# Late attention's scores in pieces of at most 512 columns, in two one-bank PSUM tiles, with a longer assumed delay of key loads

## Chip, cores, metric

One core of a Trainium2 (trn2) chip. The metric is the device time of one execution in microseconds; the kernel before was timed in three runs.

## The reference

One layer of a streaming encoder. The part that matters here is the differential attention of the prompt: 2048 frames behind 16 meta tokens, 4 heads, two softmax maps per head whose difference weights the values. A query may see every key of its own 64-frame chunk and of all earlier ones.

```python
def diff_attend(q, k, v, lam, mask):
    s = jnp.einsum('...qhcd,...khcd->...hcqk', q, k).astype(jnp.float32) * (HEAD_DIM_A ** -0.5)
    if mask is not None:
        s = jnp.where(mask, s, -jnp.inf)
    p = jax.nn.softmax(s, axis=-1)
    a = p[..., 0, :, :] - lam * p[..., 1, :, :]
    return jnp.einsum('...hqk,...khe->...qhe', a.astype(v.dtype), v)
...
    hx = hx + mix_out(oa_x, ob_x, gb_x, lw, li)
    hx = hx + ffn(hx, lw)
```

Around it stand the input projection, a gated linear attention (GLA), eight running streams of 16 frames (the sample), the output projection `mix_out` and a SwiGLU feed-forward network (FFN) of width 2816. All tensors are fp32.

## The kernel before, in words

Every product that must be exact to fp32 is made of rounded parts (`fp32r`): a high part and a low part of each operand, three products of 512 columns each (`mm3`, L203; L75 is the one line that issues all matmuls, L79 the transposes).

**Order of the work.** TensorE's (PE's) and SyncE's (SP's) instructions stand in an order that a planner in the program makes (class `Order`, L56). Streams of work are generators; each yields what it waits for next: a number of us, an event plus a delay, or a slot of a named resource. The planner keeps a virtual clock, which matmuls and transposes advance (and which jumps ahead when nothing is ready), and always goes on with the highest-ranked stream whose condition holds by that clock. The constants at L38 to L47 are the delays that it assumes. They make no instruction wait; they decide how much other PE work stands between two steps. On the chip the engines wait for each other through semaphores, and each engine runs its own instructions in order. The order on VectorE (DVE), ScalarE (ACT) and GpSimd (POOL) is made by the framework's scheduler.

**Two main streams.** `stream()` (L567) does the four projections, half of the output projection, and then the FFN in four groups of tokens, A1, A2, B1, B2 (L616 to L625). `attention()` (L533) does the sample, then the prompt's attention in three instances of class `Attention`: query blocks 0 to 3 (528 keys), blocks 4 to 7 (1040 keys), and, once the projections are done, blocks 8 to 15 (2064 keys). This last one, the late attention (L1557), runs beside the output projection, the last GLA units and the FFN of A1 and A2; after it comes the second half of the output projection, for which B1 waits.

**One unit of attention** is a head h and a block i of 128 queries; W = 16 + 128(i+1) keys. `scores` (L800) cuts W into pieces of at most 1024 columns, in each of the two maps m: blocks 8 to 14 have two pieces of 584, 648, ... 968 columns, block 15 has three of 688. Each piece takes the slot "S" of the planner, whose assumed time of use is `lat[0]`, and the PSUM tile `S`, 1024 columns wide (two banks), of which there is one:

```python
                for b, (c0, c1) in enumerate(pieces):
                    yield ("res", "S", self.lat[0])
                    S = self.ps.tile([P, 1024], F32, tag="S", bufs=1, name=f"S{h}_{i}_{m}_{b}")
```

PE writes the piece as chunks of up to 512 columns, two products a chunk (with the keys' high part `kh` and low part `kl`), and in the unit's last piece of a map one of 64 columns that masks (`big`, `ind`). Then DVE takes the row's minimum (L827) and ACT the exponential with the row sum (L828, followed by a read of the accumulator). Only then may the next piece overwrite `S`. `combine` (L834) brings the pieces to one maximum: eight small operations on `st`, then for each piece one ACT scaling of map 1 (L857) and one DVE sum into map 0 (L858). `output` (L862) comes `lat[1]` later: transposes (`at`), copies by ACT (L883) and products with the values (`ao`). A unit's scores wait until the output of the unit two before is done (`pbufs`, L898).

**Keys.** `load_k` (L761) issues eight DMAs for a head and map (two halves of the keys, high and low part, each into both halves of the partitions) and posts an event; the first scores of that map stand at least `L_KS` = 2.37 of virtual time behind it (L814). The keys of the next head are loaded when block 15 has been issued.

**FFN.** The gate and up products go into PSUM tiles `pg` and `pu`, one of each; weights come by DMA into `wrg`, `wru`, `wrd`, are rounded by ACT (L1398) and their rest is taken by POOL (L1399); `pd` is the down product, added to `h` by DVE (L1459). `tph` are the transposes of a group's normed input `hn`.

Of the kernel before, what the change touches and what calls it, by code (L numbers as in the profile page):

```python
# [9 lines left out]
F32 = mybir.dt.float32  # L10
# [9 lines left out]
P = 128  # L20
# [17 lines left out]
L_G0 = 14.55  # L38
L_G = 2.77, 2.08, 2.69
L_E = 4.5, 9.94, 1.75  # L40
L_L = 4.19, 12.69, 2.7
L_Y, L_Y0 = 9.97, 17.89
L_H = 2.66
L_V, L_Q, L_KS = 2.89, 2.08, 2.37
L_W, L_ST, L_STX, L_GP, L_GL = 0.68, 2.12, 2.19, 2.49, 5.29
L_K, L_K0 = 2.1, 0.92
L_TR, L_X, L_QK, L_KD, L_FTR = 3.13, 1.82, 12.48, 5.25, 2.97  # L47
# [8 lines left out]
class Order:  # L56
# [8 lines left out]
    def matmul(self, out, lhsT, rhs, **kw):  # L65
        n = 1
        for d in list(out.shape)[1:]:
            n *= d
        m = lhsT.shape[-1]
        if lhsT.dtype == F32R:  # L70
            self.now += max(n / 2400, m / 1200)
        else:
            c = max(n / 600, m / 600)
            self.now += c / 4 if "tile_position" in kw else c
        self.nc.tensor.matmul(out, lhsT, rhs, **kw)  # L75
# [52 lines left out]
def hymba_kernel(ctx: ExitStack, tc: tile.TileContext, I: dict, O: dict, stop: int = 9):  # L128
# [3 lines left out]
    order = Order(nc)  # L132
# [614 lines left out]
    class Attention:  # L747


        def __init__(self, pool, ps, nk, blocks, pbufs, vbufs, lat):  # L750
            self.pool, self.ps, self.nk, self.blocks = pool, ps, nk, blocks
            self.pbufs, self.vbufs, self.lat = pbufs, vbufs, lat
            self.k, self.q, self.vs = {}, {}, {}
            self.ready = {}
            self.vmz = pool.tile([P, 512], F32, name=f"vmz{nk}")
            nc.gpsimd.memset(self.vmz, 0.0)
            dma(self.vmz[0:NMETA], new_v[0:NMETA])
            self.qseq = [(h, g) for h in range(H) for g in range(blocks[0] // 2, blocks[-1] // 2 + 1)]
            self.units = [(h, i) for h in range(H) for i in blocks]
# [40 lines left out]
        def scores(self, h, i):  # L800
            pm = self.pool
            q = self.q[h, i // 2][:, :, (i % 2) * P:(i % 2 + 1) * P]
            W = NMETA + (i + 1) * P
            np_ = -(-W // 1024)
            step = -(-W // np_)
            pieces = [(c, min(c + step, W)) for c in range(0, W, step)]
            st = pm.tile([P, 40], F32, tag="st", bufs=4, name=f"st{h}_{i}")
            mn = st[:, 0:2 * np_].rearrange("p (m b) -> p m b", m=2)
            sm = st[:, 6:6 + 2 * np_].rearrange("p (m b) -> p m b", m=2)
            yield ("ev", ("q", self.nk, h, i // 2), L_Q)  # L810
            pr = [pm.tile([P, self.nk], F32, tag=f"p{m}", bufs=self.pbufs[m], name=f"p{m}_{h}_{i}")
                  for m in range(2)]
            for m in range(2):
                yield ("ev", ("k", self.nk, h, m), L_KS)  # L814
                kh, kl = self.k[h, m]
                for b, (c0, c1) in enumerate(pieces):
                    yield ("res", "S", self.lat[0])
                    S = self.ps.tile([P, 1024], F32, tag="S", bufs=1, name=f"S{h}_{i}_{m}_{b}")
                    for a0 in range(c0, c1, 512):
                        a1 = min(a0 + 512, c1)  # L820
                        m0 = max(a0, W - CHUNK)
                        o = S[:, a0 - c0:a1 - c0]
                        matmul(o, q[:, m, :], kh[:, a0:a1], start=True, stop=False)
                        matmul(o, q[:, m, :], kl[:, a0:a1], start=False, stop=m0 >= a1)
                        if m0 < a1:
                            matmul(S[:, m0 - c0:a1 - c0], ind, big[:, 0:a1 - m0], start=False, stop=True)
                    nc.vector.tensor_reduce(out=mn[:, m, b:b + 1], in_=S[:, 0:c1 - c0], axis=AX.X, op=ALU.min)  # L827
                    nc.scalar.activation(pr[m][:, c0:c1], S[:, 0:c1 - c0], AF.Exp, bias=mn[:, m, b:b + 1],  # L828
                                         scale=-1.0, accum_out=sm[:, m, b:b + 1])
                if i == self.blocks[-1] and h + 1 < H:  # L830
                    spawn(self.load_k(h + 1, m), 0, ("att", self.nk))
            return pieces, st, mn, sm, pr, W

        def combine(self, ctx_):  # L834
            pieces, st, mn, sm, pr, W = ctx_
            np_ = len(pieces)
            if np_ == 1:
                rz, r = st[:, 12:14], st[:, 14:15]
                nc.vector.reciprocal(rz, sm.rearrange("p m b -> p (m b)"))
                nc.vector.scalar_tensor_tensor(out=r, in0=sm[:, 0, :], scalar=nlam, in1=rz[:, 1:2],  # L840
                                               op0=ALU.mult, op1=ALU.mult)
                nc.vector.scalar_tensor_tensor(out=pr[0][:, 0:W], in0=pr[1][:, 0:W], scalar=r, in1=pr[0][:, 0:W],
                                               op0=ALU.mult, op1=ALU.add)
                return pr[0], rz[:, 0:1]
            mo, z, rz = st[:, 12:14], st[:, 14:16], st[:, 16:18]
            f = st[:, 18:18 + 2 * np_].rearrange("p (m b) -> p m b", m=2)
            fz = st[:, 24:24 + 2 * np_].rearrange("p (m b) -> p m b", m=2)
            nc.vector.tensor_reduce(out=mo, in_=mn, axis=AX.X, op=ALU.min)
            nc.vector.tensor_tensor(out=f, in0=mo.unsqueeze(2).to_broadcast([P, 2, np_]), in1=mn, op=ALU.subtract)
            nc.scalar.activation(f, f, AF.Exp)  # L850
            nc.vector.tensor_tensor(out=fz, in0=f, in1=sm, op=ALU.mult)
            nc.vector.tensor_reduce(out=z, in_=fz, axis=AX.X, op=ALU.add)
            nc.vector.reciprocal(rz, z)
            nc.vector.tensor_tensor(out=rz, in0=rz, in1=lamv, op=ALU.mult)
            nc.vector.tensor_tensor(out=f, in0=f, in1=rz.unsqueeze(2).to_broadcast([P, 2, np_]), op=ALU.mult)
            for b, (c0, c1) in enumerate(pieces):
                nc.scalar.activation(pr[1][:, c0:c1], pr[1][:, c0:c1], AF.Identity, scale=f[:, 1, b:b + 1])  # L857
                nc.vector.scalar_tensor_tensor(out=pr[0][:, c0:c1], in0=pr[0][:, c0:c1], scalar=f[:, 0, b:b + 1],  # L858
                                               in1=pr[1][:, c0:c1], op0=ALU.mult, op1=ALU.add)
            return pr[0], ones  # L860
# [51 lines left out]

        def run(self):
            g = ("att", self.nk)
            order.slots("S", 1)
            spawn(self.all_outputs(), 2, g)
            spawn(self.all_scores(), 1.5, g)
            yield ("idle", g)
# [600 lines left out]
    def pools(name, side):  # L1519
        return (tc.alloc_tile_pool(name=name, bufs=1, side=side),  # L1520
                tc.alloc_tile_pool(name=name + "_ps", bufs=1, space=PSUM, side=side))
# [11 lines left out]
    def attention():  # L1533

        yield ("ev", ("proj", 0), 4.0)
        pm, ps = pools("smp", "left")
        yield from make_sample(pm, ps)
        close(ps, pm, qbp)
        glap, glaps = pools("gla", "left")
        gl[:] = [glaps, glap]  # L1540
        spawn(make_gla(glap, [lambda nm: glaps.tile([P, 512], F32, tag="b1", bufs=1, name=nm)]), 2, "gla")
        pm, ps = pools("att0", "left")
        yield from Attention(pm, ps, NMETA + 512, list(range(4)), pbufs=(3, 2), vbufs=2,
                             lat=L_E).run()
        close(ps, pm)
        pm, ps = pools("att1", "left")
        yield ("ev", ("proj", 1), 6.0)
        yield from Attention(pm, ps, NMETA + 1024, list(range(4, 8)), pbufs=(3, 1), vbufs=3,
                             lat=L_E).run()
        close(ps, pm)  # L1550
        po, pps = pools("outa", "left")
        po2s[:] = [po]
        outa[:] = po, pps, output_projection(po, pps, 1, first, out_weights(po, 1, first, 1, 4.0), 2, 1, 2, po2s)
        post("early")
        yield ("ev", ("px",), 4.0)
        pm, ps = pools("att", "right")
        yield from Attention(pm, ps, NMETA + SEQ, list(range(8, NT)), pbufs=(2, 1), vbufs=4,  # L1557
                             lat=L_L).run()
        close(ps, pm)
        po, pps = pools("outb", "right")  # L1560
        for part in (1, 0):
            w = out_weights(po, part, second, 4, 3.0)
            yield from output_projection(po, pps, part, second, w, 3, 1, 2)
        close(pps, po)
        post("outb")
# [113 lines left out]
```

## Time and profile before

| | us |
|---|---|
| median of three runs | 3137.93 (3133.88 to 3143.64) |
| the profiled execution | 3135.83 |
| its span, first to last instruction | 3134.0 |
| PE busy | 2988.7 |
| DVE busy | 1463.4 |
| ACT busy | 1210.4 |
| mean granted clock of TensorE | 0.982 of full |

The profile is of one execution. Its page gives each engine's busy time, the chain of work that ended last and groups of instructions; the trace behind it answers for any stretch: who waited for whom, the instructions in order of time, and busy times with the granted clock. A wait is idle time of an engine just before an instruction, put down to what released it. The late attention lies between 977 us (its first score) and 1906 us.

### The profile page before, as it was taken

The numbers are of one execution on the slowest core, as the hardware profiler recorded it, in microseconds if no ns is written. First come the engines' busy times: TensorE is split into PE (matmuls) and PEld (weight loads), VectorE is DVE, ScalarE is ACT, GpSimd is POOL, SyncE is SP. The second block draws the span as 40 slices with busy tenths as digits, with TensorE's granted clock in tenths as the row PEclk, the third lists the DMA queues.
The fourth block names the chain that finished last, engine by engine and source line by source line (L and its number), as shares of the span: only waits on it lengthen the run. The fifth ranks groups of instructions, "written<-read, shape, count | busy, mean of one in ns | idle before, by whom it ended". The sixth has DMA issues, their size and how long they took to land. (4 is left out here: it accounts for less than half of the span.)

```text
span 3134.0 us, 41977 instructions
## 1 busy us (share of the span) xinstructions
PE 2988.7 (95%) x16049; PEld 2492.6 (80%) x16049; DVE 1463.4 (47%) x2506; ACT 1210.4 (39%) x2270; POOL 953.5 (30%) x530
## 2 busy tenths in 40 slices
PE   8999999999998896999999999999999999999999
PEld 5776778787776785887877887788788877999998
DVE  6445346556653653544445654643333333333333
ACT  5444434455541544544434543322322223222221
POOL 2012112122251102323322335424444444333332
PEclk9999999999998998999999999999999999999999
DMA  4437676546368437225234324643333334322222
GB/s 158 126 129 221 215 212 174 172 149 190 105 215 207 144 131 196 88 68 136 74 80 137 127 72 149 200 161 108 121 122 93 100 109 133 102 73 77 81 69 73
DMA packets 411358, 415.22 MB, mean 132 GB/s; under 512 B 34547, under 2 KB 303029, under 8 KB 411157
## 3 DMA queue, kind: packets, MB, share of 16 engines
q1 hardware_dynamic: 372372, 384.26, 40.5%
q10 hardware_dynamic: 38528, 28.26, 2.8%
q8 instruction: 127, 2.08, 0.3%
q14 instruction: 75, 0.61, 0.1%
q0 software_dynamic: 256, 0.01, 0.0%
HBM read 334.02 MB, written 78.42 MB: 132 GB/s over the span
## 5 line engine op out<-in xcount | busy, mean ns | idle before, releaser
L1459 DVE TENSOR_TENSOR h<-h,pd 128x512 f32<-128x512 f32 x374 | 255.9, 685 | 460.5 <-PE pd L75 460.0
L1399 POOL TENSOR_TENSOR wgl<-wrg,wgh 128x1024 fp32r<-128x1024 f32 x88 | 216.4, 2459 | 497.8 <-PE pu L75 343.2
L1399 POOL TENSOR_TENSOR wul<-wru,wuh 128x1024 fp32r<-128x1024 f32 x88 | 214.2, 2434 | 447.7 <-PE pg L75 335.8
L75 PE MATMUL pg<-nh,wgh 128*128 128x512 f32 (+1 forms) x880 | 324.7, 369 | 6.8 <-DVE sg L201 6.8
L75 PE MATMUL pu<-nh,wuh 128*128 128x512 f32 (+1 forms) x880 | 321.8, 366 | 0.0
L75 PE MATMUL pg<-nl,wgh 128*128 128x512 f32 (+1 forms) x880 | 318.1, 361 | 0.0
L75 PE MATMUL pg<-nh,wgl 128*128 128x512 f32 (+1 forms) x880 | 317.5, 361 | 0.0
L75 PE MATMUL pu<-nl,wuh 128*128 128x512 f32 (+1 forms) x880 | 315.9, 359 | 0.0
L75 PE MATMUL pu<-nh,wul 128*128 128x512 f32 (+1 forms) x880 | 315.6, 359 | 0.0
L75 PE MATMUL pd<-wdh,th 128*128 128x512 f32 x748 | 296.8, 397 | 5.4 <-DVE h L1459 4.2
L75 PE MATMUL pd<-wdh,tl 128*128 128x512 f32 x748 | 293.6, 393 | 0.0
L75 PE MATMUL pd<-wdl,th 128*128 128x512 f32 x748 | 292.4, 391 | 0.0
L827 DVE TENSOR_REDUCE st<-S 128x1 f32<-128x688 f32 (+13 forms) x208 | 179.6, 863 | 223.7 <-PE S L75 222.0
L828 ACT ACTIVATE p<-S,st 128x688 f32<-128x688 f32 (+13 forms) x208 | 172.3, 829 | 230.2 <-DVE st L827 228.5
L1399 POOL TENSOR_TENSOR wdl<-wrd,wdh 128x1024 fp32r<-128x1024 f32 x88 | 225.9, 2567 | 102.6 <-ACT wdh L1398 102.4
L1448 ACT CAST th<-sg 128x512 fp32r<-128x512 f32 (+1 forms) x110 | 61.3, 557 | 403.2 <-DVE sg L1446 403.1
L75 PEld LDWEIGHTS pg<-nh,wgh 128*128 128x128 f32 x880 | 167.1, 190 | 29.6 <-DVE sg L201 8.0
L75 PEld LDWEIGHTS pg<-nh,wgl 128*128 128x128 f32 x880 | 166.6, 189 | 23.4
L75 PEld LDWEIGHTS pg<-nl,wgh 128*128 128x128 f32 x880 | 167.1, 190 | 21.2
L75 PEld LDWEIGHTS pu<-nh,wul 128*128 128x128 f32 x880 | 165.1, 188 | 22.5
L75 PEld LDWEIGHTS pu<-nh,wuh 128*128 128x128 f32 x880 | 165.3, 188 | 21.1
L75 PEld LDWEIGHTS pu<-nl,wuh 128*128 128x128 f32 x880 | 165.5, 188 | 20.7
(396 smaller groups left out, 6358.8 us busy)
## 6 DMA issues: line engine op xcount, KB each, us to landing
wrg<-in_w_ffn_gate_dram SPq DMA_DIRECT2D x88, 512.0 KB, 4.0
wru<-in_w_ffn_up_dram SPq DMA_DIRECT2D x88, 512.0 KB, 3.9
wrd<-in_w_ffn_down_dram SPq DMA_DIRECT2D x88, 512.0 KB, 3.4
h_d<-xr SPq DMA_DIRECT2D x34, 512.0 KB, 3.8
xr<-h_d SPq DMA_DIRECT2D x17, 512.0 KB, 4.0
hn<-h_d SPq DMA_DIRECT2D x17, 512.0 KB, 4.5
h<-h_d SPq DMA_DIRECT2D x17, 512.0 KB, 7.0
out_dram<-h SPq DMA_DIRECT2D x17, 512.0 KB, 3.1
```

The source lines that it names most:

```text
L75: self.nc.tensor.matmul(out, lhsT, rhs, **kw)
L827: nc.vector.tensor_reduce(out=mn[:, m, b:b + 1], in_=S[:, 0:c1 - c0], axis=AX.X, op=ALU.min)
L828: nc.scalar.activation(pr[m][:, c0:c1], S[:, 0:c1 - c0], AF.Exp, bias=mn[:, m, b:b + 1], scale=-1.0, accum_out=sm[:, m, b:b + 1])
L1399: nc.gpsimd.tensor_tensor(out=b, in0=raw, in1=r32(a), op=ALU.subtract)
L1448: nc.scalar.copy(th[:, c0:c0 + n], sg)
L1459: nc.vector.tensor_tensor(out=hs[n][:, e], in0=hs[n][:, e], in1=ps, op=ALU.add)
```

## The change

Late attention gets pieces of at most 512 columns and two PSUM tiles of one bank each, and the planner two slots "S", each with an assumed time of use of 4.6 instead of 4.19. The pieces' width is rounded up to a multiple of 8, and the statistics tile `st` has room for five pieces. The assumed delay from a key load's issue to its first scores, which all three instances use, becomes 5.5 instead of 2.37.

```diff
-L_L = 4.19, 12.69, 2.7
+L_L = 4.6, 12.69, 2.7
...
-L_V, L_Q, L_KS = 2.89, 2.08, 2.37
+L_V, L_Q, L_KS = 2.89, 2.08, 5.5
...
-        def __init__(self, pool, ps, nk, blocks, pbufs, vbufs, lat):
+        def __init__(self, pool, ps, nk, blocks, pbufs, vbufs, lat, width=1024, sbufs=1):
+            self.width, self.sbufs = width, sbufs
...
-            np_ = -(-W // 1024)
-            step = -(-W // np_)
+            np_ = -(-W // self.width)
+            step = -(-W // (8 * np_)) * 8
             pieces = [(c, min(c + step, W)) for c in range(0, W, step)]
-            st = pm.tile([P, 40], F32, tag="st", bufs=4, name=f"st{h}_{i}")
+            st = pm.tile([P, 48], F32, tag="st", bufs=4, name=f"st{h}_{i}")
...
-                    S = self.ps.tile([P, 1024], F32, tag="S", bufs=1, name=f"S{h}_{i}_{m}_{b}")
+                    S = self.ps.tile([P, self.width], F32, tag="S", bufs=self.sbufs, name=f"S{h}_{i}_{m}_{b}")
...
-            order.slots("S", 1)
+            order.slots("S", self.sbufs)
...
-                             lat=L_L).run()
+                             lat=L_L, width=512, sbufs=2).run()
```

Left out are the new column numbers of the parts of `st`. For blocks 8 to 15 the pieces of a map become 3, 3, 3, 4, 4, 4, 4 and 5, of 384 to 488 columns; before they were 2 (seven times) and 3. Over 4 heads and 2 maps that is 240 pieces instead of 136. The two earlier instances keep their pieces.

What moves on PE, first between two pieces of head 1, block 14 (`S1_14_m_b` is map m, piece b; `pu` and `pg` are products of the FFN beside it). Before:

```order
L75 MATMUL S1_14_0_0_12613<-kh2064_1_0_11194,qs1_7_12180 128x512
L75 MATMUL S1_14_0_0_12613<-kl2064_1_0_11195,qs1_7_12180 128x512
L75 MATMUL S1_14_0_0_12613<-kh2064_1_0_11194,qs1_7_12180 128x456
L75 MATMUL S1_14_0_0_12613<-kl2064_1_0_11195,qs1_7_12180 128x456
L75 MATMUL pu0_6_0_12525<-nh0_11227,wuh19_12399 128x512
...
L75 MATMUL pg0_7_0_12631<-nh0_11227,wgl20_12474 128x512
L75 MATMUL S1_14_0_1_12651<-kh2064_1_0_11194,qs1_7_12180 128x512
```

Now:

```order
L75 MATMUL S1_14_0_0_12795<-kh2064_1_0_11320,qs1_7_12331 128x488
L75 MATMUL S1_14_0_0_12795<-kl2064_1_0_11321,qs1_7_12331 128x488
L75 MATMUL S1_14_0_1_12800<-kh2064_1_0_11320,qs1_7_12331 128x488
L75 MATMUL S1_14_0_1_12800<-kl2064_1_0_11321,qs1_7_12331 128x488
L75 MATMUL pg0_7_0_12761<-nh0_11275,wgh20_12572 128x512
...
L75 MATMUL pg0_7_0_12761<-nh0_11275,wgl20_12573 128x512
L75 MATMUL S1_14_0_2_12831<-kh2064_1_0_11320,qs1_7_12331 128x488
```

In both, 18 products of 512 columns of the FFN stand where the dots and the rows beside them are; before, they lie between one piece and the next, now between one pair of pieces and the next pair.

Second, the start of head 1 (block 8), where FFN group A1 begins (`pg0_0_0` and `pu0_0_0`). Before, 12 products of `pg0_0_0` stand between the last piece of map 0 and the first of map 1:

```order
L75 MATMUL S1_8_0_1_11416<-big_175,ind_172 128x64
L75 MATMUL pg0_0_0_11426<-nh0_11227,wgh1_11251 128x512
...
L75 MATMUL pg0_0_0_11426<-nh0_11227,wgl1_11252 128x512
L75 MATMUL S1_8_1_0_11441<-kh2064_1_1_11337,qs1_4_10839 128x512
L75 MATMUL S1_8_1_0_11441<-kl2064_1_1_11338,qs1_4_10839 128x512
```

Now:

```order
L75 MATMUL S1_8_0_2_11537<-big_175,ind_172 128x64
L75 MATMUL pg0_0_0_11505<-nh0_11275,wgh1_11299 128x512
...
L75 MATMUL pu0_0_0_11546<-nh0_11275,wul2_11414 128x512
L79 MATMUL at0_15_0_11569<-ident_165,p0_0_15_11210 128x128 x4
L75 MATMUL pu0_0_0_11546<-nh0_11275,wuh2_11413 128x512
...
L75 MATMUL pu0_0_0_11546<-nh0_11275,wul2_11414 128x512
L75 MATMUL S1_8_1_0_11589<-kh2064_1_1_11467,qs1_4_10934 128x392
```

Now 27 such products and four transposes stand there.

Third, the start of the late attention on PE, at head 0, map 1 (`po1` are products of the output projection). Before:

```order
L75 MATMUL po1_3_1_9730<-woh1_0_2_8787,yl1_3_9558 128x512
L75 MATMUL S0_8_1_0_9740<-kh2064_0_1_9604,qs0_4_9455 128x512
L75 MATMUL S0_8_1_0_9740<-kl2064_0_1_9605,qs0_4_9455 128x512
L75 MATMUL S0_8_1_0_9740<-kh2064_0_1_9604,qs0_4_9455 128x72
L75 MATMUL S0_8_1_0_9740<-kl2064_0_1_9605,qs0_4_9455 128x72
L75 MATMUL gsc13_9753<-QS1_3905,gkf13_9539 64x64 x8
L75 MATMUL po1_3_1_9730<-woh1_0_3_8927,yh1_3_9557 128x512
```

Now:

```order
L75 MATMUL po1_3_1_9721<-woh1_0_2_8958,yl1_3_9558 128x512
L75 MATMUL gsc13_9747<-QS1_3905,gkf13_9539 64x64 x8
L75 MATMUL po1_3_1_9721<-woh1_0_3_9113,yh1_3_9557 128x512
L75 MATMUL po1_3_1_9721<-wol1_0_3_9114,yh1_3_9557 128x512
L75 MATMUL po1_3_1_9721<-woh1_0_3_9113,yl1_3_9558 128x512
L75 MATMUL po1_4_0_9761<-woh1_0_0_8757,yh1_4_9657 128x512
L75 MATMUL po1_4_0_9761<-wol1_0_0_8758,yh1_4_9657 128x512
L75 MATMUL po1_4_0_9761<-woh1_0_0_8757,yl1_4_9658 128x512
L79 MATMUL tpy1_5_0_9767<-ident_165,y1_5_9566 128x128 x4
L75 MATMUL S0_8_1_0_9774<-kh2064_0_1_9604,qs0_4_9455 128x392
```

The first scores of map 1 moved behind eight small matmuls of the GLA, six products of the output projection and four transposes. In the two earlier instances the first scores of a map also move behind more of the projections' products; head 0's scores of the 1040 keys move from behind the third part of `pnv2_0` to behind most of `pnv2_3`.

## Rows read from the trace of the kernel before

**Rows 1.** The page, busy time of the engines (share of the span, instructions).

```profile
PE 2988.7 (95%) x16049; PEld 2492.6 (80%) x16049; DVE 1463.4 (47%) x2506; ACT 1210.4 (39%) x2270; POOL 953.5 (30%) x530
```

**Rows 2.** PE's waits, 0 to 975 us: total, times, longest.

```profile
PE S L75 <- DMA kl<-kTl_d: 5.9, 5, 1.9
...
PE S L75 <- DMA kh<-kTh_d: 4.8, 4, 2.2
```

**Rows 3.** PE's waits, 975 to 1220 us.

```profile
PE S L75 <- ACT p L828: 9.0, 5, 4.3
PE tph L79 <- DVE hss L194: 7.4, 1, 7.4
PE S L75 <- DMA kl<-kTl_d: 7.1, 3, 2.5
...
PE S L75 <- DMA kh<-kTh_d: 2.8, 1, 2.8
```

**Rows 4.** PE's waits, 1220 to 1910 us.

```profile
PE S L75 <- ACT p L828: 17.9, 10, 5.3
```

**Rows 5.** Timeline of PE, first scores of 1040 keys: start, duration, idle before.

```profile
600.63 0.47 PE L75 MATMUL S<-kh,qs 128*128 128x512 f32 x1 [1.55 <-DMA kh<-kTh_d]
602.67 0.76 PE L75 MATMUL S<-kl,qs 128*128 128x512 f32 x1 [1.56 <-DMA kl<-kTl_d]
...
606.05 0.46 PE L75 MATMUL S<-kl,qs 128*128 128x144 f32 x1 [1.92 <-DMA kl<-kTl_d]
```

**Rows 6.** Timeline of ACT around 1412 us: a cast, then a piece's exponential.

```profile
1411.88 1.05 ACT L1398 CAST wuh<-wru 128x1024 fp32r<-128x1024 f32 x1 [7.25 <-DMA wru<-in_w_ffn_up_dram]
1412.83 0.83 ACT L828 ACTIVATE p<-S,st 128x688 f32<-128x688 f32 x1
```

**Rows 7.** Stretches: PE, PEld, DVE, ACT, POOL busy; then PE clock, DMA share, GB/s.

```profile
600.00:615.00 15.00, 10.67 (x32) 8.03 (x33) 3.77 (x8) 2.08 (x4) 1.35 (x1) 0.66 0.93 263
...
980.00:1012.00 32.00, 23.33 (x92) 18.07 (x92) 10.54 (x23) 8.21 (x27) 6.44 (x7) 0.68 1.06 279
...
1414.00:1419.00 5.00, 5.00 (x21) 4.39 (x21) 1.20 (x2) 0.23 (x1) 1.43 (x1) 0.66 0.61 125
1591.00:1600.00 9.00, 6.28 (x20) 5.15 (x21) 3.93 (x5) 4.75 (x8) 1.72 (x1) 0.62 0.20 58
```

**Rows 8.** Timeline of PE around 1223 us: the rest of a 584-column piece, full clock.

```profile
1223.08 0.39 PE L75 MATMUL S<-kl,qs 128*128 128x512 f32 x1
1223.31 0.20 PE L75 MATMUL S<-kh,qs 128*128 128x72 f32 x1
1223.35 0.27 PE L75 MATMUL S<-kl,qs 128*128 128x72 f32 x1
1223.45 0.28 PE L75 MATMUL S<-big,ind 128*128 128x64 f32 x1
```

**Rows 9.** Groups on ACT by shape, 980 to 1910 us: count, busy us, mean ns.

```profile
L828 ACT ACTIVATION_READ_ACCUMULATOR p<-S,st 128x1 f32 x136 | 26.3, 193 | 0.0
...
L828 ACT ACTIVATE p<-S,st 128x968 f32<-128x968 f32 x16 | 17.1, 1069 | 33.4 <-DVE st L827 33.4
...
L828 ACT ACTIVATE p<-S,st 128x584 f32<-128x584 f32 x16 | 11.9, 747 | 9.2 <-DVE st L827 9.2
...
L857 ACT ACTIVATE p<-p,st 128x968 f32<-128x968 f32 x8 | 8.4, 1098 | 5.3 <-DVE st L855 5.3
...
L857 ACT ACTIVATE p<-p,st 128x584 f32<-128x584 f32 x8 | 5.8, 776 | 2.3 <-DVE st L855 2.3
```

**Rows 10.** Groups on DVE by shape, 980 to 1910 us.

```profile
L827 DVE TENSOR_REDUCE st<-S 128x1 f32<-128x968 f32 x16 | 18.6, 1164 | 9.2 <-PE S L75 9.1
...
L827 DVE TENSOR_REDUCE st<-S 128x1 f32<-128x584 f32 x16 | 12.2, 764 | 21.5 <-PE S L75 21.4
...
L858 DVE SCALAR_TENSOR_TENSOR p<-p,st,p 128x776 f32<-128x776 f32 x8 | 8.0, 1022 | 1.0 <-ACT p L857 1.0
L858 DVE SCALAR_TENSOR_TENSOR p<-p,st,p 128x712 f32<-128x712 f32 x8 | 7.4, 954 | 2.5 <-ACT p L857 2.5
```

More of the change, by code (lines that the diff above doesn't have):

```diff
@@ L803, in scores @@
             W = NMETA + (i + 1) * P
-            np_ = -(-W // 1024)
-            step = -(-W // np_)
+            np_ = -(-W // self.width)
+            step = -(-W // (8 * np_)) * 8
             pieces = [(c, min(c + step, W)) for c in range(0, W, step)]
-            st = pm.tile([P, 40], F32, tag="st", bufs=4, name=f"st{h}_{i}")
+            st = pm.tile([P, 48], F32, tag="st", bufs=4, name=f"st{h}_{i}")
             mn = st[:, 0:2 * np_].rearrange("p (m b) -> p m b", m=2)
-            sm = st[:, 6:6 + 2 * np_].rearrange("p (m b) -> p m b", m=2)
+            sm = st[:, 10:10 + 2 * np_].rearrange("p (m b) -> p m b", m=2)
             yield ("ev", ("q", self.nk, h, i // 2), L_Q)
@@ L837, in combine @@
             if np_ == 1:
-                rz, r = st[:, 12:14], st[:, 14:15]
+                rz, r = st[:, 20:22], st[:, 22:23]
                 nc.vector.reciprocal(rz, sm.rearrange("p m b -> p (m b)"))
@@ L844, in combine @@
                 return pr[0], rz[:, 0:1]
-            mo, z, rz = st[:, 12:14], st[:, 14:16], st[:, 16:18]
-            f = st[:, 18:18 + 2 * np_].rearrange("p (m b) -> p m b", m=2)
-            fz = st[:, 24:24 + 2 * np_].rearrange("p (m b) -> p m b", m=2)
+            mo, z, rz = st[:, 20:22], st[:, 22:24], st[:, 24:26]
+            f = st[:, 26:26 + 2 * np_].rearrange("p (m b) -> p m b", m=2)
+            fz = st[:, 36:36 + 2 * np_].rearrange("p (m b) -> p m b", m=2)
             nc.vector.tensor_reduce(out=mo, in_=mn, axis=AX.X, op=ALU.min)
```

## The prediction

> **What bounds the kernel.** I read the page's busy times first. PE is busy for 2988.7 of 3134.0 us, DVE for less than half of it and ACT for 39% [rows 1]. So the end is set by PE's products and by PE's waits, and a change pays only if it takes products or waits off PE. Next I read whom PE waits for, stretch by stretch, and kept what scores wait for. Before 975 us they wait 5.9 + 4.8 = 10.7 us for key loads [rows 2]. Between 975 and 1220 us, where the late attention begins, they wait 7.1 + 2.8 = 9.9 us for keys and 9.0 us for an exponential, that is, for the one tile S to come free [rows 3]. From 1220 to 1910 us ten waits for the exponential take 17.9 us, the longest 5.3 [rows 4]. These 47.5 us are what the change can reach.
>
> Then I looked at what such a wait is made of. The key waits come in chains: at 600 to 606 us the products wait 1.55, 1.56 and 1.92 us for one part of the keys after another [rows 5]. The slot waits come from ACT's or DVE's own queue. At 1412 us ACT stands 7.25 us before a cast of FFN weights, whose load has not landed, and a piece's exponential, queued behind that cast, runs only at 1412.83 [rows 6]. Last, the clock: around these waits PE is granted 0.62 to 0.68 of full on average; at 1414 to 1419 us PE is busy all 5 us, but granted only 0.66, so part of the stretch is at 1.2 GHz instead of 2.4 [rows 7].
>
> **The change, part by part.**
>
> *Products.* The columns stay the same, the chunks become fewer and even. A product of 512 columns starts 0.23 us before the next (1223.08 to 1223.31). The two of 72 columns take 0.04 + 0.10 us [rows 8], though 72 columns at that pace are 0.032 each: the pair loses 0.075 us. Chunks of 264 columns and more lose nothing that I can see. Blocks 8, 9 and 10 have two short chunks a map, block 15 three: 9 × 8 = 72 pairs, with losses from 0.075 us down to some 0.03: 2 to 5 us, of which I take 4. **-4.**
>
> *Key loads.* The first scores of a head's map now stand 5.5 - 2.37 = 3.13 us later in the plan, with other products before them. PE has such products at every place in question (projections in the first two instances, the output projection in the third), so a wait shrinks by what moved ahead. The early 10.7 us lie at three places: at 600 us 1.55 + 1.56 + 1.92 with a little between (5.2), the rest near 400 and 780 us, about 2.7 each. The first loses 3.1, the others all: -8.5 to -9. In the late instance the 9.9 us shrink less. The order puts eight small matmuls, six products and four transposes ahead of map 1's first piece, but other work that stood ahead now stands behind, and I count 2.5 us net. The loads there are held by the DMA engines, which are busy throughout (share 1.06, 279 GB/s [rows 7]). I take 3. **-12**, between 0 and -20.6.
>
> *The slots.* A piece of 968 columns frees its tile after a reduce of 1.16 us and an exponential of 1.07 [rows 9, 10]: 2.2 us after its last product. Between it and the next piece stand 18 products, 18 × 0.23 = 4.1 us. So 1.9 us of lateness are free, and the rest PE waits. In the new order two pieces stand together, and both tiles are wanted again after the same 18 products. What changes is the chain. A reduce costs 156 ns and 1.04 ns a column, an exponential 257 ns and 0.84 ns a column (from the lines of 584 and 968 columns [rows 9, 10]). At 488 columns that is 0.66 + 0.67 us. The first piece of a pair is free 1.3 us after its products. The second also waits for the first one's exponential and accumulator read, about 1.75 us. Each has 4.6 us until its tile is wanted (the 18 products and the other piece's two). The free lateness becomes 3.3 and 2.8 us instead of 1.9: 0.9 to 1.4 more, say 1.1. Ten waits, each 1.1 shorter and none below zero: -9 of the 17.9. Of the 9.0 us before 1220, the longest wait of 4.3 is map 1 of head 1's first block: 27 products and four transposes now stand there instead of 12, some 4 us more, so it goes; the other four keep about 4. -5. **-14**, between +10 (the added work below comes into the chain) and -26.9.
>
> *The clock.* If waits go, some stretches at the lower level go. The four shown lose 5.1, 10.2, 1.7 and 3.4 us by length times missing share [rows 7]. The one at 980 us stays, as its waits mostly do. Half of the others: **-5**, between 0 and -20.
>
> *Added work.* 240 - 136 = 104 more pieces, and 120 - 68 = 52 more parts in combine. On ACT: 104 × (257 + 193) ns and 52 × 286 ns (L857, from the same two widths) = 62 us. On DVE: 104 × 156 ns, and 52 × 0.2 us for L858 (from 712 and 776 columns), = 26 us. ACT is busy for 39% of the span and DVE for 47% [rows 1], a little more in this stage, so most of it lies beside PE's work. Combine has more and shorter parts, but ACT and DVE take turns in it, and 12.69 us are planned from the last piece to the transposes; PE waits nowhere for that now after 975 us. If the cover fails, ACT's 62 us is the price. I take **+2**.
>
> The Trainium skill, VectorE: DVE Perf Modes, in its section on the TRN2 errata, says that a fixed latency is exposed between instructions, so that many small tiles pay it each, and advises tiles of 512 elements or more. That speaks against pieces of 384 to 488 columns. The fixed parts above are what the lines here show of it. By that rule alone the change costs these 62 and 26 us and the sum is rival D's; by rows 1 they are beside PE, and it is mine.
>
> *Sum.* -4 - 12 - 14 - 5 + 2 = -33 from the profiled execution's 3135.8: 3102.8. That execution is 2.1 us under the median, well inside the runs' spread of 10, so I say **3104**. About 0.3% (9.4 us) is what a measurement of this kernel can tell from no change.
>
> **Rivals.**
>
> *A, the pairs bring nothing.* Both tiles of a pair hang on the same ACT queue. When that queue stands for 7.25 us [rows 6], 3 us of free lateness is soon gone, and the next cast may catch two pieces instead of one. Then the slot waits and the clock stay, and half of the key gain: -4 - 6 + 2 = -8 gives 3129 (placed below the median as above), no change that can be told. For it: the chain's causes are untouched. Against: the waits now average 1.8 us, in the reach of 1.1. The Trainium skill, TensorE: Matmul & The Clock Gate, section HAM oscillation — how this bites in real kernels, tells of a matmul kernel that gained nothing further from double-buffered PSUM. No run here shows it; by that rule the time would be this rival's.
>
> *B, the loads take it back.* At the start of FFN group A1 PE waits 7.4 us for a normed input [rows 3], whose load it cannot hurry, and at 980 us for keys under a full DMA. If PE only comes earlier to both, what was saved before 1220 us is lost there: the early key gain of 9 and 6 more. 3104 + 15 = 3119.
>
> *C, all goes.* Every wait of scores and all four slow stretches vanish: -4 - 20.6 - 26.9 - 20 + 2 = -69.5, 3068. Against: the full DMA at 980 us.
>
> *D, slower.* ACT's queue becomes the bound in the late attention: 62 us more in an in-order queue that already stands for loads. FFN's gate tile, of which there is one, waits for ACT and DVE to read it, so each delay there reaches PE. From some 45 us of the added 62 on PE's path the gain of 35 is turned into a loss of over 0.3%; all of it gives 3104 + 60 = 3164. Against: ACT is idle more often than not [rows 1], and the gate's reads hold PE up nowhere between 975 and 1910 us now.
>
> **Chances.** Forecast 0.61 (its own range 3088 to 3120), A 0.14, B 0.12, C 0.06, D 0.07. Faster by over 0.3% is below 3128.5: forecast, B and C, 0.79. Same: A, 0.14. Slower: D, 0.07. The range takes in A above and half of the unknown gains below, 3080 to 3131, and leaves out C and D.
>
> **What would show it.** Right: fewer than 16 us of PE's waits for the exponential behind scores after 975 us; key waits near 9 us in all, nearly all of them around 980 to 1010; 240 exponentials of 580 to 670 ns in the late attention; ACT busy some 60 us more, and no new waits of PE for `p` of L858 or for the gate's reads. Wrong: those waits unchanged (A), longer waits at `tph` (B), or a PE that waits for ACT in the FFN (D).

## The result and the profile after

| | us |
|---|---|
| before, beside the changed kernel | 3137.18 (3133.88 to 3143.64) |
| changed kernel, median of four runs | 3098.87 (3098.39 to 3103.0) |
| ratio, 95% interval | 0.9874 [0.9856, 0.9892] |
| the profiled execution of the changed kernel, its span | 3103.0, 3101.3 |
| mean granted clock | 0.985 of full (before 0.982) |

The change takes 38 us off by the medians, 32.7 us between the two profiled spans (3134.0 to 3101.3). The latter is what the traces can account for; it is the smaller of the two, since the profiled execution of the changed kernel is the slowest of its four. Lines behind L750 of the program stand one further down than before (L828 is now L829).

The page's busy times:

```profile
PE 2976.2 (96%) x15985; PEld 2486.5 (80%) x15985; DVE 1465.6 (47%) x2662; ACT 1242.8 (40%) x2530; POOL 950.9 (31%) x530
```

Against [rows 1] PE is busy 12.5 us less, and so 20.2 us of the 32.7 were idle time. ACT has 260 instructions more, but only 32 us more busy time.

PE's waits of the changed kernel from 0 to 975 us (total, times, longest), beside [rows 2]:

```profile
PE pnvb L75 <- POOL wlvb L385: 4.3, 4, 2.0
PE S L75 <- DMA kl<-kTl_d: 3.4, 4, 1.5
...
PE S L75 <- DMA kh<-kTh_d: 2.5, 1, 2.5
```

From 975 to 1220 us, beside [rows 3]:

```profile
PE po L75 <- DVE xr L1314: 7.6, 2, 4.8
PE tph L79 <- DVE hn L1377: 6.5, 1, 6.5
PE ao L75 <- ACT aT L884: 5.8, 3, 2.4
...
PE S L75 <- DMA kl<-kTl_d: 2.9, 1, 2.9
PE S L75 <- ACT p L829: 2.6, 4, 1.3
PE S L75 <- DMA kh<-kTh_d: 1.6, 1, 1.6
```

From 1220 to 1910 us, beside [rows 4]:

```profile
PE S L75 <- ACT p L829: 7.9, 6, 2.0
PE ao L75 <- ACT aT L884: 5.9, 5, 2.2
```

Read together: the key waits fell from 20.6 to 3.4 + 2.5 + 2.9 + 1.6 = 10.4 us. The waits for the exponential behind scores fell from 9.0 + 17.9 to 2.6 + 7.9 = 10.5 us after 975 us (over the whole span from 27.3 to 12.4). Other waits grew: `ao`, which waits for the copies of the transposed scores, from 9.0 to 15.0 us over the span, and the output projection, which waits for its residual `xr`, from 3.5 to 9.2 us.

The stretches of [rows 7], and one more, in the changed kernel (PE, PEld, DVE, ACT, POOL busy, then PE clock, DMA share, GB/s):

```profile
600.00:615.00 15.00, 15.00 (x78) 12.57 (x78) 3.53 (x8) 5.11 (x10) 2.16 (x2) 1.00 0.66 197
622.00:629.00 7.00, 4.35 (x12) 3.46 (x13) 2.18 (x3) 3.01 (x6) 1.27 (x1) 0.52 1.09 303
...
980.00:1012.00 32.00, 24.66 (x112) 18.89 (x112) 12.09 (x33) 9.17 (x33) 7.12 (x6) 0.73 1.05 289
...
1414.00:1419.00 5.00, 5.00 (x26) 4.14 (x25) 4.33 (x9) 2.63 (x6) 0.92 (x1) 1.00 1.06 250
1591.00:1600.00 9.00, 9.00 (x47) 7.65 (x46) 3.21 (x7) 4.03 (x9) 4.61 (x2) 1.00 0.20 59
```

At 600, 1414 and 1591 us PE now has the full clock and no idle time. The two late stretches did not merely move: from 1216 to 1910 us the mean clock is 1.00 instead of 0.99. The stretch at 980 us stays slow (0.73 instead of 0.68), and the one of 600 us has moved with its waits to 622 us.

The busy time of the scores' products alone, 975 to 1910 us (length, PE busy, then clock, DMA share, GB/s), first before, then changed:

```profile
975.00:1910.00 935.00, 132.21 (x608) 0.97 0.41 120
```

```profile
975.00:1910.00 935.00, 127.26 (x544) 0.97 0.43 126
```

With 64 products fewer the scores take 5.0 us less.

One place shows what a slot wait is made of. Here is ACT in the changed kernel (start, duration, idle before it), at a place like that of [rows 6]:

```profile
1401.23 1.04 ACT L1399 CAST wgh<-wrg 128x1024 fp32r<-128x1024 f32 x1 [7.33 <-DMA wrg<-in_w_ffn_gate_dram]
1402.18 0.60 ACT L829 ACTIVATE p<-S,st 128x416 f32<-128x416 f32 x1
1402.68 0.19 ACT L829 ACTIVATION_READ_ACCUMULATOR p<-S,st 128x1 f32 x1
1402.78 0.60 ACT L829 ACTIVATE p<-S,st 128x416 f32<-128x416 f32 x1
```

And the piece that waits for it on PE, in the changed kernel:

```profile
1402.93 0.46 PE L75 MATMUL S<-kh,qs 128*128 128x416 f32 x1 [1.42 <-ACT p L829]
```

In the kernel before, behind the cast of [rows 6]:

```profile
1413.80 0.50 PE L75 MATMUL S<-kh,qs 128*128 128x512 f32 x1 [2.58 <-ACT p L828]
```

The cause is untouched: ACT still stands 7.33 us before a cast whose weights have not landed, now with a pair of pieces queued behind it. But PE waits 1.2 us less for it. Only 0.2 of that is the shorter exponential, which ends 1.55 us behind the cast's start instead of 1.78. The rest is that PE comes to the tile 0.3 us after the cast has begun instead of 0.7 us before it (start less wait: 1401.51 and 1411.22). One place depends on when a load happens to land, so the reading rests on the totals and on the runs below.

### The profile page after: what moved, and what is told of

It is laid out like the page before. It is cut to its first block, busy times and chain, and to the rows that moved or that the text cites. A ratio compares the mean times of both kernels' runs of the same rounds, so it can differ in the third digit from the quotient of the medians.

```text
span 3101.3 us, 42273 instructions
## 1 busy us (share of the span) xinstructions
PE 2976.2 (96%) x15985; PEld 2486.5 (80%) x15985; DVE 1465.6 (47%) x2662; ACT 1242.8 (40%) x2530; POOL 950.9 (31%) x530
## 5 line engine op out<-in xcount | busy, mean ns | idle before, releaser
L829 ACT ACTIVATE p<-S,st 128x392 f32<-128x392 f32 (+13 forms) x312 | 197.7, 636 | 199.0 <-DVE st L828 198.1
L828 DVE TENSOR_REDUCE st<-S 128x1 f32<-128x392 f32 (+13 forms) x312 | 187.0, 623 | 165.8 <-PE S L75 165.2
```

## The experiments

All were timed in five rounds beside the kernel before, whose median lay between 3136.9 and 3140.3 us; so experiments are compared by their ratios to it. Waits are PE's over the whole span, unless said otherwise. None changes what is computed.

**The longer key delay alone.**

```diff
-L_V, L_Q, L_KS = 2.89, 2.08, 2.37
+L_V, L_Q, L_KS = 2.89, 2.08, 5.5
```

> The kernel before with the longer assumed delay of key loads alone (5.5 instead of 2.37); the late scores keep pieces of up to 1024 columns and their one tile. Theory (the prediction's terms add up): the key waits lose 12 us and the clock some 2 to 3, the waits for the exponential stay at about 27 us over the span: 14 us off the kernel before, ratio about 0.9955, 3123 us beside a before of 3137. Rival B (the loads take it back): the early waits shrink by 7 to 9 us, but the time by 5 us or less, since PE waits longer behind the next load, ratio 0.998 or above. Second rival (the delay does all of it): 30 us or more off, ratio 0.990 or below, and the waits for the exponential shrink too.

Measured 3127.66 us, ratio 0.9963 [0.9951, 0.9974]: 11.4 us off. PE's waits:

```profile
PE S L75 <- ACT p L828: 31.7, 23, 7.4
...
PE S L75 <- DMA kl<-kTl_d: 7.7, 5, 3.2
PE S L75 <- DMA kh<-kTh_d: 4.9, 2, 2.6
```

The keys' waits go from 20.6 to 12.6 us, 8 us less where the theory had 12, and the slots' waits do not shrink. Rival B and the second rival fall; the key delay is a part of its own.

**Pieces and two tiles alone** (the changed kernel with the old key delay).

```diff
-L_V, L_Q, L_KS = 2.89, 2.08, 5.5
+L_V, L_Q, L_KS = 2.89, 2.08, 2.37
```

> The changed kernel with the old delay of key loads (2.37): pieces of at most 512 columns and two one-bank tiles alone. Theory (the terms add up): products -4, slots -14, clock -2 to -3, added work +2: 19 us off the kernel before, ratio about 0.994, 3118 us; the waits for the exponential after 975 us near 10 us as in the changed kernel, the key waits near 20 us as before. Rival A (the pairs bring nothing): within 8 us of the kernel before, ratio 0.9975 or above. Second rival (the delay does none of it): as the changed kernel, ratio 0.988.

Measured 3120.68 us, ratio 0.9941 [0.992, 0.9962]: 18.4 us off.

```profile
PE S L75 <- DMA kh<-kTh_d: 14.5, 5, 8.7
...
PE S L75 <- DMA kl<-kTl_d: 11.1, 8, 2.7
PE S L75 <- ACT p L829: 8.4, 8, 4.8
```

The slots' waits fall as in the changed kernel. The keys' waits do not: they grow from 20.6 to 25.6 us, 8.7 of it before map 1 of head 0's first block. So the longer key delay takes 15.2 us of such waits off the pairs (25.6 to 10.4) and only 8.0 off the one tile. The two parts add to 30 us; both together gave 38. With the intervals as they are (0.4% and 0.6%, against 1.26%, each uncertain by 0.1 to 0.2%), whether the time has more than the sum is open, though these waits point that way.

**Short pieces, but one tile of one bank**, at the same planned rate (from the changed kernel).

```diff
-L_L = 4.6, 12.69, 2.7
+L_L = 2.3, 12.69, 2.7
...
-                             lat=L_L, width=512, sbufs=2).run()
+                             lat=L_L, width=512, sbufs=1).run()
```

> The changed kernel with one one-bank tile instead of two, and the planned spacing of pieces halved (2.3 instead of 4.6), so that the pieces come at the same rate but one by one. A piece's chain of reduce and exponential is 1.3 us, the products between two pieces some 2 us: the free lateness is 0.8 us, less than before (1.9). Theory (the free lateness decides): the waits for the exponential come back and grow past those of before, 27 us or more after 975 us, and the time is 15 us or more above the changed kernel, 3114 us or above. Rival (short pieces do it, the second tile nothing): the waits stay near 12 us and the time within 5 us of the changed kernel.

Measured 3155.33 us, ratio 1.0055 [1.0035, 1.0075]: slower than the kernel before, and 56 us above the changed one.

```profile
PE S L75 <- ACT p L829: 66.4, 48, 5.1
```

At this rate of short pieces the second tile is worth all of the gain and more. The rival falls.

**One tile of two banks, only planned further apart** (from the kernel before).

```diff
-L_L = 4.19, 12.69, 2.7
+L_L = 5.5, 12.69, 2.7
```

> The kernel before with more planned spacing of its one tile alone (5.5 instead of 4.19); pieces, tile and key delay as before. Some 24 products would stand between two pieces instead of 18, so the free lateness is 5.5 - 2.2 = 3.3 us, as that of the two tiles. Theory (lateness alone decides, whatever gives it): the waits for the exponential after 975 us fall to about 10 to 12 us, and the time by some 10 to 14 us, ratio about 0.996, if the attention's scores still find enough other products to stand among. Rival (a second tile is needed): no gain, within 5 us of before, or a loss, because the late attention is stretched and the output projection or the FFN behind it starts later.

Measured 3120.78 us, ratio 0.9943 [0.9924, 0.9963]: not to be told from pieces and two tiles, and more than the 10 to 14 us of the theory.

```profile
PE S L75 <- ACT p L828: 12.5, 8, 5.1
```

For these waits a second tile is not needed: one number does it, with no instruction added. The rival falls.

**Both numbers, without pieces or second tile** (the kernel before with key delay 5.5 and spacing 5.5).

> The kernel before with the two planned delays alone: key loads 5.5 instead of 2.37, and the spacing of its one late tile 5.5 instead of 4.19. Pieces, chunks and tile are those before. Theory (lateness decides, from whatever source, and the terms add up): the runs with one of the two alone stand 11.5 and 18.3 us under the kernel before, so 30 us off, ratio about 0.9905, 3109 us; the key waits near 10 us, the waits for the exponential after 975 us near 12. Rival (both take the same stretch of late attention and spread it twice, so part is paid again behind it): 20 us off or less, ratio 0.9935 or above. Second rival (the second tile is needed for part of it that adds up no other way): the changed kernel's ratio of 0.9874 is out of reach by 10 us or more; the theory leaves it some 8 us, of which the fewer short chunks are 4 to 5.

Measured 3109.45 us, ratio 0.9901 [0.9881, 0.992]; slots' waits 11.9 us, keys' 9.3. This is the sum to the microsecond. What is left to the changed kernel is 8.5 us by the ratios, 10.6 by the medians, so the theory's 8 and the second rival's 10 can't be told apart; the intervals of the two ratios just overlap. The page says where it lies:

```profile
PE 2986.2 (96%) x16049; PEld 2493.5 (80%) x16049; DVE 1462.8 (47%) x2506; ACT 1208.0 (39%) x2270; POOL 948.4 (30%) x530
```

PE is busy 10.0 us longer than in the changed kernel, and its idle time, 126.3 us of a span of 3112.5, is nearly that of the changed kernel (125.1). So beside two numbers the pieces and the second tile bring no fewer waits in all. They bring less busy time: 2.6 us of scores' products (129.9 to 127.3 in the late attention), and the rest with a mean clock of 0.985 instead of 0.982.

**Wider pairs** (the changed kernel with spacing 6.0).

```diff
-L_L = 4.6, 12.69, 2.7
+L_L = 6.0, 12.69, 2.7
```

> The changed kernel with the spacing of its two tiles at 6.0 instead of 4.6. Theory: the free lateness grows by another 1.4 us, the waits for the exponential after 975 us fall from 10.5 us to 4 or less, and the time by 4 to 8 us, to 3091 to 3095. Rival (the spacing has its price: the late attention is stretched, its last blocks find no other products to stand among, and the output projection behind it starts later): the same or slower, 3099 to 3110.

Measured 3104.04 us, ratio 0.9887 [0.9869, 0.9906].

```profile
PE pg L75 <- DVE sg L201: 14.4, 4, 7.6
PE tph L79 <- DVE nl L218: 10.5, 5, 4.6
...
PE S L75 <- ACT p L829: 3.0, 5, 1.0
```

The theory was right about the waits (3.0 us). The time did not follow: it is that of the changed kernel within the intervals, as the rival said. The last late score comes at 1901 us instead of 1833, and PE waits in the FFN instead: for the gate 14.4 us (6.7 in the changed kernel), for `nl` 10.5 (2.7).

**More work for ACT** (the changed kernel, rival D put to the test).

```diff
                     nc.scalar.activation(pr[m][:, c0:c1], S[:, 0:c1 - c0], AF.Exp, bias=mn[:, m, b:b + 1],
                                          scale=-1.0, accum_out=sm[:, m, b:b + 1])
+                    if self.sbufs == 2:
+                        nc.scalar.activation(pr[m][:, c0:c0 + 232], pr[m][:, c0:c0 + 232], AF.Identity,
+                                             scale=ones)
```

> The changed kernel with one more ACT operation behind each of the 240 exponentials of the late attention: a multiplication of 232 columns of the piece by one, in place, some 0.45 us each, 108 us of ACT in all. It does not change the result. Theory (ACT's added work lies beside PE's): 3 to 15 us slower than the changed kernel, through the queue alone: the second exponential of a pair is 0.45 us later (waits for the exponential 10.5 to about 15 us) and the copies of the transposed scores too; 3102 to 3114 us. Rival D (ACT's queue is the bound in this stage): 60 us slower or more, 3160 us or above.

Measured 3101.89 us, ratio 0.9883 [0.9865, 0.9901]. The added group on ACT, 970 to 1945 us (busy, mean ns):

```profile
L832 ACT ACTIVATE p<-p,ones 128x232 f32<-128x232 f32 x240 | 112.7, 488 | 0.7
```

PE's waits:

```profile
PE ao L75 <- ACT aT L887: 17.3, 15, 4.0
PE S L75 <- ACT p L829: 10.1, 12, 2.0
```

ACT is busy for 1331.3 us, 88.5 more, and the time is that of the changed kernel within the interval. Rival D falls. The medians differ by 3.0 us, the theory's lower end, which the interval can't tell from nothing.

**A longer key delay still** (the changed kernel with 8.0).

```diff
-L_V, L_Q, L_KS = 2.89, 2.08, 5.5
+L_V, L_Q, L_KS = 2.89, 2.08, 8.0
```

> The changed kernel with the assumed delay of key loads at 8.0 instead of 5.5. Theory (key waits shrink by the work put ahead, as far as there is any): the 5.9 us before 975 us go, the 4.5 us of the late instance halve: 5 to 8 us less, 3091 to 3094. Rival (the DMA engines hold the late keys, and the products moved ahead have run out): the key waits stay, or PE waits as long for the next load behind them: within 3 us of the changed kernel, or slower.

Measured 3102.37 us, ratio 0.9884 [0.9865, 0.9902]. The keys' waits fall from 10.4 to 2.9 us, a single wait. So the waits went as the theory said, not as the rival did, but the median did not follow (3.5 us above the changed kernel). Slots' waits are 14.5 us instead of 12.4. The profiled spans say otherwise (3095.6 against 3101.3), but there the fastest of six executions stands beside the slowest of four; with an interval of 6 us to each side, what became of the 7.5 us is open.

**A longer delay of the copies of the transposed scores** (the changed kernel with `lat[2]` 4.0 instead of 2.7).

> The changed kernel with the planned delay between the transposes of a group of scores and the products that read their copy (aT) at 4.0 instead of 2.7 in the late attention. It goes at what is left: eight waits of PE for that copy after 975 us, 11.7 us, the longest 2.4. Theory (lateness again: each wait 1.3 us shorter, none below zero): 8 to 9 us less, about 3090 us, ratio 0.985. Rival (as with the wider pairs: the tiles that the output holds, one for the transposes and one for its products, come free later, the attention is stretched, and the waits turn up elsewhere): within 4 us of the changed kernel.

Measured 3102.04 us, ratio 0.9876 [0.9859, 0.9893]. The wait aimed at halves (15.0 to 7.0 us), and the time stays within the interval: `tph` waits 10.9 us for `nl`, and 9.2 once for nothing that the profile shows. The rival holds; the last late score comes at 1901 us here too.

**Three delays at once** (the changed kernel with spacing 5.2, key delay 8.0, copies 4.0).

> The changed kernel with three delays a little longer: spacing of the pairs 5.2, key loads 8.0, copy of the transposed scores 4.0. Theory (each wait left is a matter of lateness): waits for the exponential 10.5 to about 6 us, for aT 11.7 to about 3, keys as before: 3085 to 3092 us. Rival (the late attention's stretch has only so many other products; what it spreads further it lacks at its end or start): 3096 us or above.

Measured 3091.77 us (3086.31 to 3095.66), ratio 0.9845 [0.9827, 0.9864]: the theory's upper end. The slots' waits are 4.7 us, those for `aT` 6.7, the keys' 3.1; which number gives it the last run tells.

**Pairs at the spacing of before** (the changed kernel with 4.19).

```diff
-L_L = 4.6, 12.69, 2.7
+L_L = 4.19, 12.69, 2.7
```

> The changed kernel with the spacing of its two tiles left at the 4.19 of before instead of 4.6, to split that number off from the second tile and the short pieces. Theory (the chain, not the number, gives most): the free lateness is 0.4 us less, ten waits grow by 0.4 us each: 2 to 5 us above the changed kernel, 3101 to 3104. Rival (the spacing gives most, as with the one tile, where 1.3 us more of it gave 18 us off): 6 us or more above it, 3105 us or higher, waits for the exponential 15 us or more.

Measured 3117.12 us, ratio 0.9928 [0.9912, 0.9945].

```profile
PE S L75 <- ACT p L829: 19.6, 16, 3.1
...
PE tph L79 <- DVE hn L1377: 9.7, 1, 9.7
...
PE tph L79 <- issue: 7.5, 1, 7.5
```

The rival holds. With the key delay in both, pairs at 4.19 gain some 11 us over one tile at 4.19 (0.9963 to 0.9928), and 0.41 of spacing gains 17 more by the ratios (0.9928 to 0.9874); by their intervals I estimate some 8 us of uncertainty in the 17. The profiled spans differ by 8.9 us (3110.2 to 3101.3), 7.2 of it in the slots' waits, but they set the fastest execution of one against the slowest of the other. The other five runs at 4.19 had a clock of 0.980 to 0.983, the changed kernel's had 0.985 to 0.986, so part of the 17 may be the clock.

**Pairs at 5.2 alone.**

```diff
-L_L = 4.6, 12.69, 2.7
+L_L = 5.2, 12.69, 2.7
```

> The changed kernel with the spacing of its two tiles alone at 5.2 instead of 4.6, one of the three numbers of the run with all delays a little longer (3091.8 us). Theory (the spacing has a best value between 4.6 and 6.0, and it gave that run's gain): waits for the exponential after 975 us fall from 10.5 to 4 to 6 us, 3090 to 3096 us. Rival (no single number gives it, as the key delay of 8.0 and the copy's 4.0 gave nothing alone): 3098 to 3105 us, the waits moved to the FFN's input or the copies of the transposed scores.

Measured 3090.2 us (3087.18 to 3094.97), ratio 0.9858 [0.9833, 0.9882]. PE's waits:

```profile
PE S L75 <- ACT p L829: 7.8, 11, 2.4
```

After 975 us the waits are 6.5, a little above the 4 to 6 forecast. The last late score starts at 1853 us, 20 later than in the changed kernel. The time is as the theory had it: this number alone gives what the run of three gave. All runs of this kernel and of that one are below all runs of the changed kernel (3098.39 to 3103.0), though the intervals of the ratios overlap. They are the fastest of the study. That 5.2 is better than 4.6 or 6.0 is therefore likely, not shown; only the run of three, also at 5.2, has an interval wholly below that of 6.0.

**All spacings side by side**, all with the key delay at 5.5. The distance is what the order of PE's instructions puts between a tile's last product and the first product of its next piece: the median over the late pieces, each product counted at its time at full clock. The free lateness is the distance less the chain of reduce and exponential (for the widest pieces: 2.2 us for a long one, 1.3 for a single short one, 1.5 as the mean of a pair).

| tiles, spacing | distance | free lateness | slots' waits | ratio |
|---|---|---|---|---|
| one short, 2.3 | 2.6 | 1.3 | 66.4 | 1.0055 |
| one long, 4.19 | 4.1 | 1.9 | 31.7 | 0.9963 |
| pairs, 4.19 | 4.55 | 3.0 | 19.6 | 0.9928 |
| one long, 5.5 | 5.55 | 3.3 | 11.9 | 0.9901 |
| pairs, 4.6 (the changed kernel) | 5.1 | 3.6 | 12.4 | 0.9874 |
| pairs, 5.2 | 5.7 | 4.2 | 7.8 | 0.9858 |
| pairs, 6.0 | 6.6 | 5.1 | 3.0 | 0.9887 |

The waits fall as the free lateness grows, whichever way it was made: by a shorter chain, a second tile or plain distance (11.9 and 12.4 are as good as equal). The time follows down to the pairs at 5.2. At 6.0 the attention is stretched so far that the FFN beside and behind it waits instead, and the time gains no more.

## Why the prediction was right, and where its steps were not

The forecast of 3104 us, 33 off, came out at 3099, inside its range; A, C and D did not happen. Against A stands also that at equal spacing the pairs gain 11 us over the one tile. That the profiled spans differ by 32.7, almost the 33 of the sum, is partly luck: terms that were off or not counted cancelled. Of the signs named, the waits behind scores (10.5 us, fewer than 16) and the absence of new waits for `p` and the gate held; ACT's 60 us more and key waits nearly all around 980 to 1010 us did not. Against its terms:

**Products: -4, measured -5.0**, by the busy times above. Over the kept profiles the same products take 129.9 to 135.0 us in long pieces and 126.2 to 129.1 in short ones.

**Slots: -14, measured -16.4** (26.9 to 10.5 us of waits after 975 us, which the term was about; -14.9 over the span). The size is about right. At the place where ACT stands 2.58 us of wait became 1.42, and 1.1 less was forecast, but that agreement proves little: 0.2 came from the chain, the rest from when PE got there beside the load's landing. And the step gave the gain to short pieces and a second tile. The runs give a good part of it to the number beside them: at 4.19 the same pairs leave 19.6 us. And the one long tile at 5.5 does as well by these waits as the pairs (11.9 and 12.4 us). The step worked with 18 products as given, though the spacing that sets their number was the cheaper lever.

**Keys: -12, measured -10.2, but from other places.** The early waits fell by 4.8 us (10.7 to 5.9) instead of 8.5 to 9, the late ones by 5.4 (9.9 to 4.5) instead of 3. The early step that failed is "a wait shrinks by what moved ahead". Of the three early places, those near 400 and 780 us did nearly vanish. The chain of [rows 5] did not; in the changed kernel it reads:

```profile
620.17 0.47 PE L75 MATMUL S<-kl,qs 128*128 128x512 f32 x1 [0.70 <-DMA kl<-kTl_d]
623.15 0.49 PE L75 MATMUL S<-kh,qs 128*128 128x144 f32 x1 [2.51 <-DMA kh<-kTh_d]
625.14 0.46 PE L75 MATMUL S<-kl,qs 128*128 128x144 f32 x1 [1.50 <-DMA kl<-kTl_d]
```

4.7 us instead of 5.2. SP's queue shows a possible reason (start, duration):

```profile
614.16 1.25 SPq L772 DMA_DIRECT2D kh<-kTh_d  x2
615.46 0.58 SPq L347 DMA_DIRECT2D wrqb<-in_w_in_dram  x1
616.09 1.13 SPq L772 DMA_DIRECT2D kl<-kTl_d  x2
...
618.38 1.09 SPq L772 DMA_DIRECT2D kh<-kTh_d  x2
619.53 0.59 SPq L347 DMA_DIRECT2D wrqb<-in_w_in_dram  x1
620.16 1.08 SPq L772 DMA_DIRECT2D kl<-kTl_d  x2
```

Before, the four pairs of key loads started at 596.73, 598.64, 599.77 and 601.71, 5.0 us from first to last, with two stores between. Now the projection's products that were put ahead bring the loads of their own weights (`wrqb`) between the keys' loads, and they start over 6.0 us. The product of the last part starts 5.0 us after its load's issue instead of 4.3. The DMA engines are also fuller there: at 619 to 625 us their share is 1.03, at 600 to 606 before it was 0.88. The key delay alone shows the same chain, so it is not the pieces' doing; whether the weight loads cause it, by their place in the queue or by the DMA engines' time, is read from this order and was not tried by itself. The late gain beyond 3 us is in head 0's first block: its waits of 2.23 and 2.54 us for `kl`, at 980 and 992 us, are gone, and the two left are those of map 1 (1.57 and 2.90). The key delay alone leaves 7.1 us there, so part of the late gain comes with the pieces.

**Clock: -5, measured about -7**: PE's busy time fell by 12.5 us, 5.0 of it by products, and the rest I put down to the clock, whose mean rose from 0.982 to 0.985 (0.3% of PE's 2980 us are 9); no row shows that rest by itself. Of the four stretches named, three are at full clock now where they were, and one came with the key waits at 622 us.

**Added work: ACT +62 us, DVE +26, at a cost of 2.** The cost is right: a further 88.5 us of ACT's busy time changed nothing that the timing can tell. The sizes are right as sums of durations and too high as busy time. Count times mean of the groups grows by 61 us on ACT (last section) and by 23 on DVE (the reduce 136 × 948 to 240 × 600 ns, the sum 68 × 1220 to 120 × 760 ns). But ACT's busy time rose by 32 us, as operations overlap at their ends. DVE's busy time in these two groups rose by 12 us (128.9 to 136.5 and 81.1 to 85.7), and other groups fell, so that 2 are left. The Trainium skill, VectorE: DVE Perf Modes, section on the TRN2 errata, warns that operations that read from SBUF pay a fixed latency each, so that many small tiles pay it often. In combine, whose scaling reads SBUF, the rows agree: 613 ns at 392 columns is again 286 ns and 0.84 ns a column. The reduce and the exponential read PSUM, of which the warning does not speak. PE pays nothing that the runs can tell.

**What was not counted.** Four sums account for the 20.2 us of idle time: keys -10.2, slots -14.9, the FFN's input transposes `tph` -8.4 (24.0 to 15.6, not in the forecast), and +13.3 net in waits that the prediction costed at nothing, `ao` +6.0 and the others +7.3, `xr` +5.7 and `pnvb` +4.3 among them. So rival B was right that work which comes earlier meets inputs that are late, at the output projection rather than at `tph`. But it does not take the gain back: at the first `tph` of group A1 the changed kernel is 16.6 us ahead (1186.3 to 1169.7), at group B1's 33.3 (2197.9 to 2164.6), at the end 32.7.

## To carry to other kernels

Where an engine waits for a buffer, work out the free lateness first: the other work planned between its last use and its next, less the chain that frees it. More distance in the plan may do what a second buffer does, for one number and no added instructions; try it before, and again after, and stop where the stretched stage makes a later one wait. A planned delay does not only put work ahead of a load's consumer; here it also put that work's own loads into the queue between the parts of the load.

## What the runs showed of the hardware beyond what was expected

ACT's operations overlap at their ends, so rows of mean durations overstate short pieces. In the fence of 1401 us an exponential of 0.60 us and an accumulator read of 0.19 stand in sequence, and the next exponential starts 0.60 us after the first. From start to start the exponential takes 0.50 and the read 0.10: each runs its last 0.1 or so under the next operation. By group, 970 to 1945 us, in the kernel before:

```profile
L828 ACT ACTIVATE p<-S,st 128x688 f32<-128x688 f32 (+7 forms) x136 | 121.8, 895 | 162.8 <-DVE st L827 162.0 <-DVE st L848 0.4
L857 ACT ACTIVATE p<-p,st 128x688 f32<-128x688 f32 (+7 forms) x68 | 59.4, 924 | 24.7 <-DVE st L855 24.3 <-ACT oo L886 0.4
```

and in the changed kernel:

```profile
L829 ACT ACTIVATE p<-S,st 128x392 f32<-128x392 f32 (+6 forms) x240 | 147.2, 616 | 142.7 <-DVE st L828 142.1
L858 ACT ACTIVATE p<-p,st 128x392 f32<-128x392 f32 (+12 forms) x120 | 69.1, 645 | 26.4 <-DVE st L856 26.4
L829 ACT ACTIVATION_READ_ACCUMULATOR p<-S,st 128x1 f32 x240 | 47.0, 196 | 0.0
```

With the reads of [rows 9] these groups grow from 207.5 to 263.3 us, by 55.8 (by 61 as count times mean), near the 62 forecast, while the engine's busy time grew by 32.4. A further operation of 488 ns behind each exponential showed the same: 112.7 us by its row, 88.5 of busy time. The Trainium skill, ScalarE: Activation LUTs, in its section What ACT_TABLE_LOAD costs, says that ACTIVATEs back to back overlap by about 93 ns. The 0.10 us here agrees, between an exponential and the read of the accumulator behind it; the cast of 1401.23 us and the exponential behind it overlap by 0.09.
